# Row sums of a 16384 x 1024 array: two leads of 128 rows instead of one

## The chip, the cores and the metric

The kernel runs on one core of a Trainium2 chip. The metric is the device time of one launch in microseconds (us); where several runs are named, their median. A core has engines with instruction streams of their own: VectorE (DVE in the profile), ScalarE (ACT), GpSimd (POOL), TensorE (PE) and SyncE (SP). Data come from the chip's memory (DRAM) into the on-chip buffer, which has 128 partitions, through DMA transfers; here all of them are issued on SP, onto one queue that 16 DMA engines work through. The engines wait for each other, and for landed transfers, by semaphores.

## The reference

```python
def setup_inputs():
    batch, seq, dim = 32, 512, 1024
    return {
        "x": np.random.randn(batch, seq, dim).astype(np.float32),
        "multiplier": 0.5,
    }

def reference(x: np.ndarray, multiplier: float) -> np.ndarray:
    return (np.sum(x, axis=-1) * multiplier).astype(np.float32)
```

Each of the 16384 rows of 1024 float32 numbers is summed and multiplied by 0.5. The input has 67.11 MB, the output 65.5 KB.

## The kernel before

The rows are shared out over the 128 partitions, 128 rows to each. They are processed in blocks of B = 16 rows of a partition: 8 blocks. A full block is 64 KB in each partition, 8192 KB in all.

- Blocks 0 to 6 (loop at L114): partition p owns the 112 consecutive rows p*112 to p*112 + 111, so a block's partitions lie 448 KB apart in DRAM. Three buffers of a block each (`buf`, xb in the profile) take turns. The load of block b (`load`, L81; the issue itself is L83) waits on SP until VectorE has reduced block b - 3. VectorE sums the whole block in one instruction (`reduce_sum`, L133) into `sums` and scales the sums into `res` (L139). Of block 6 VectorE takes only the first 8 rows; ScalarE sums the other 8, one row to an instruction (`act_row`, L89, L90), with scale and sum in one.
- The lead (L113, L125 to L130): the last 128 rows of the array, one row to a partition, in one load of 512 KB that is issued ahead of all others. VectorE sums it with `dve_sum` (L98, L100), which adds one half of a row to the other and sums the result. The sums stand in a column of `lead_sq`, a tile of 128 x 32 that a memset (L111) has cleared. A transpose of 32 x 32 blocks (L128) brings them into the rows 0, 32, 64, 96 of `lead_tr`, 32 sums to a row.
- The last block has `tail` = 15 rows in a partition (partition p owns 15 consecutive rows, 60 KB apart), and comes in five loads: pieces of 9 and 4 rows (L156), a mixed one of row 13 and the first 384 columns of row 14 (`landed_mix`), and the rest of row 14 in two loads of 352 and 288 columns into the tile `end` (L169). All five wait on SP for the reduction of block 4 (L155). Rows 5 to 8 and 12 and row 13 are ScalarE's (L182, L193); the others are VectorE's, by `dve_sum`. Row 14 is summed in three parts: each partial sum is put into a column of `end` beside the next part's numbers, so the last sum, `final` (L200), contains the two before it.
- Stores: SP waits for block 6's scaled sums (L173) and stores the 112 finished sums of each partition (L174, the early store), then the lead's 128 sums as 4 rows of 32 (L178). At the end it waits for ScalarE's last row (L204) and for `final`, and stores the last block's sums (L205). L209 to L211 wait until the three stores have landed.

The function `start_loads_at_entry` puts the loads that wait for nothing (the lead and blocks 0 to 2) into the entry block on SP, ahead of the barrier at which all engines meet. So they are issued first of all; VectorE and ScalarE start after that barrier.

The order on SP is then: lead, blocks 0, 1, 2; blocks 3, 4, 5, 6, each behind its wait; the five loads of the last block; the early store; the lead's store; the last store.

Of the kernel before, what the change touches and what calls it, by code (L numbers as in the profile page):

```python
# [9 lines left out]
def kernel(  # L10
# [13 lines left out]
    nc = tc.nc  # L24
# [4 lines left out]
    P = nc.NUM_PARTITIONS  # L29
# [4 lines left out]
    N, D = x_flat.shape  # L34
    rows = N // P
    out_flat = out.rearrange("b s -> (b s)")
    mul = float(multiplier)

    B = 16
    n_blocks = rows // B  # L40
    assert N == P * rows and rows == n_blocks * B
    own = rows - B
    tail = B - 1
    lead0 = P * (own + tail)
    x_rows = x_flat[0 : P * own, :].rearrange("(p c) d -> p c d", p=P)
    x_last = x_flat[P * own : lead0, :].rearrange("(p c) d -> p c d", p=P)
    x_lead = x_flat[lead0:N, :]
    out_rows = out_flat[0 : P * own].rearrange("(p c) -> p c", p=P)
    out_last = out_flat[P * own : lead0].rearrange("(p c) -> p c", p=P)
    out_lead = out_flat[lead0:N].rearrange("(q c) -> q c", c=32)  # L50

    def sbuf(name, *shape):
        return ctx.enter_context(nc.sbuf_tensor(name, list(shape), fp32)).ap()
# [4 lines left out]
    res = sbuf("res", P, rows)  # L58
    cut = (384, 736)
    at = 352  # L60
    end = sbuf("end", P, at + 2 + D - cut[1])
    S = 32
    lead = sbuf("lead", P, D)
    lead_sq = sbuf("lead_sq", P, S)
    lead_tr = sbuf("lead_tr", P, S)

    def sem(name):
        return nc.alloc_semaphore(name=name)
# [5 lines left out]
    def marks(i, engine):  # L74

        s = dve_done if engine == "dve" else act_done
        i.then_inc(s, 1)
        counts[engine] += 1
        return counts[engine]

    def load(name, dst, src, free=None):  # L81
        landed = sem(name)
        i = nc.sync.dma_start(out=dst, in_=src)  # L83
        if free is not None:
            i.wait_op(dve_done, free, "sem-ge")
        i.then_inc(landed, 16)
        return landed

    def act_row(t, r, col):  # L89
        return nc.scalar.activation(  # L90
            out=t[:, r, :],
            in_=t[:, r, :],
            func=mybir.ActivationFunctionType.Copy,
            scale=mul,
            accum_out=res[:, col : col + 1],
        )

    def dve_sum(row, dst, scale):  # L98
        mid = row.shape[-1] // 2
        return nc.vector.tensor_tensor_reduce(  # L100
            out=row[:, 0:mid],
            in0=row[:, 0:mid],
            in1=row[:, mid:],
            scale=scale,
            scalar=0.0,
            op0=ADD,
            op1=ADD,
            accum_out=dst,
        )

    zeroed = marks(nc.vector.memset(lead_sq, 0.0), "dve")  # L111
    freed = []
    lead_landed = load("lead_landed", lead, x_lead)  # L113
    for b in range(n_blocks - 1):  # L114
        c0 = b * B
        t = buf[b % bufs]
        landed = load(
            f"landed{b}",
            t,
            x_rows[:, c0 : c0 + B, :],  # L120
            freed[b - bufs] if b >= bufs else None,
        )
        h = B if b < n_blocks - 2 else B // 2
        if b == 0:
            nc.vector.wait_ge(lead_landed, 16)  # L125
            nc.vector.wait_ge(dve_done, zeroed)
            summed = marks(dve_sum(lead, lead_sq[:, 0:1], mul), "dve")
            turned = nc.vector.transpose(out=lead_tr, in_=lead_sq)  # L128
            turned.wait_op(dve_done, summed, "sem-ge")
            marks(turned, "dve")  # L130
        nc.vector.wait_ge(landed, 16)
        done = marks(
            nc.vector.reduce_sum(  # L133
                out=sums[:, c0 : c0 + h], in_=t[:, 0:h, :], axis=mybir.AxisListType.X
            ),
            "dve",
        )
        freed.append(done)
        scaled = nc.vector.tensor_single_scalar(  # L139
            out=res[:, c0 : c0 + h],  # L140
            in_=sums[:, c0 : c0 + h],
            scalar=mul,
            op=mybir.AluOpType.mult,
        )
        scaled.wait_op(dve_done, done, "sem-ge")
        early_dve = marks(scaled, "dve")
        if h < B:
            nc.scalar.wait_ge(landed, 16)
            for r in range(h, B):
                i = act_row(t, r, c0 + r)  # L150
            early_act = marks(i, "act")
# [1 line left out]
    c0 = (n_blocks - 1) * B  # L153
    t = buf[(n_blocks - 1) % bufs]
    nc.sync.wait_ge(dve_done, freed[n_blocks - 1 - bufs])  # L155
    pieces = [(0, 9), (9, 13)]  # L156
    landed = [
        load(f"landed_p{k}", t[:, lo:hi, :], x_last[:, lo:hi, :])
        for k, (lo, hi) in enumerate(pieces)
# [15 lines left out]
    early.wait_op(act_done, early_act, "sem-ge")  # L175
    early_stored = sem("early_stored")
    early.then_inc(early_stored, 16)
    lead_store = nc.sync.dma_start(out=out_lead, in_=lead_tr[0:P:S, :])  # L178
    lead_stored = sem("lead_stored")
    lead_store.then_inc(lead_stored, 16)  # L180

    on_act = {5, 6, 7, 8, 12}  # L182
    for k, (lo, hi) in enumerate(pieces):
        on = [r for r in range(lo, hi) if r in on_act]
        nc.scalar.wait_ge(landed[k], 16)
# [11 lines left out]
    part = dve_sum(end[:, 0:at], end[:, at + 1 : at + 2], 1.0)  # L197

    part.then_inc(landed_end[1], 1)
    final = dve_sum(end[:, at:], res[:, rows - 2 : rows - 1], mul)  # L200
    final.wait_op(landed_end[1], 17, "sem-ge")
    done = marks(final, "dve")

# [3 lines left out]
    stored = sem("stored")  # L207
    store.then_inc(stored, 16)
    nc.sync.wait_ge(early_stored, 16)  # L209
    nc.sync.wait_ge(lead_stored, 16)  # L210
    nc.sync.wait_ge(stored, 16)  # L211

    def start_loads_at_entry(nc_):
# [61 lines left out]
```

## Time and profile before

| | |
|---|---|
| Time, median of 3 runs | 160.63 us (160.52 to 160.78) |
| Profiled execution, its own time | 160.85 us |
| Its span, first to last instruction | 159.5 us |
| VectorE idle before block reductions (L133), waiting for loads | 30.5 us, 7 times |
| ScalarE idle, waiting for loads | 138.8 us, 4 times |
| Read from DRAM, mean rate over the span | 67.11 MB, 421 GB/s |

The profile is of one execution. Its span is shorter than the time of the run, which also contains what lies before the first and after the last instruction. In the lines of the profile, a row of the timeline gives start, duration, engine, line, operation, output and input with their shapes, how many instructions are merged into the row, and in brackets the idle time before it and what ended it. "SPq" is the issue of a DMA on SP; its duration is that of the issue, not of the transfer. A row of the chain gives start, duration and what it was. A row of DMA issues gives how often, the size and the time from issue to landing. "CUSTOM_DVE_ANT_0" is the instruction of `dve_sum`.

### The profile page before, as it was taken

To read this page: it belongs to the slowest core of one execution; us is meant where nothing else is said; L and a number is where in the kernel's file an instruction comes from. 1 tells how busy PE (TensorE), PEld (TensorE's weight loads), DVE (VectorE), ACT (ScalarE), POOL (GpSimd) and SP (SyncE) were. 2 spreads that over 40 slices of the span, in tenths; PEclk is the share of its full clock that TensorE was granted. 3 is DMA by queue.
4 is the path that set the end of the run, shared out by engine and by line. 5 is a ranking of instruction groups with operands and counts; after the bars stand their busy time and mean duration, and the time that the engine had idled before them with its cause. 6 is when DMAs were issued, how large, how long until landed. Compare 5 with 4: busy or idle time off the path is not lost.

```text
span 159.5 us, 129 instructions
## 1 busy us (share of the span) xinstructions
DVE 120.2 (75%) x40; ACT 16.3 (10%) x29; POOL 0.2 (0%) x4
## 2 busy tenths in 40 slices
DVE  2000029999499995999869997799959999599456
ACT  2000000000000000000000000000000000099384
POOL 0000000000000000000000000000000000000000
DMA  9969979999699699699898996996996996999994
GB/s 394 526 263 526 477 312 526 394 394 526 279 509 526 263 526 493 296 526 411 378 526 362 427 526 279 509 526 263 526 526 263 526 526 263 411 444 444 407 405 141
DMA packets 2168, 67.18 MB, mean 421 GB/s; under 512 B 504, under 2 KB 760, under 8 KB 1016
## 3 DMA queue, kind: packets, MB, share of 16 engines
q1 hardware_dynamic: 2168, 67.18, 98.0%
HBM read 67.11 MB, written 0.07 MB: 421 GB/s over the span
## 4 chain that ended last, share of the span: by engine, by line
DMA 75%; DVE 24%; SPq 1%; issue 0%
DMA xb<-in_x_dram 75%; DVE sums L133 22%; DVE xb L100 1%; SPq L83 1%; DVE end L100 0%; DVE res L139 0%; DVE res L100 0%
## 5 line engine op out<-in xcount | busy, mean ns | idle before, releaser
L133 DVE TENSOR_REDUCE sums<-xb 128x16 f32<-128x16384 f32 (+1 forms) x7 | 112.0, 16001 | 30.5 <-DMA xb<-in_x_dram 30.5
L90 ACT ACTIVATE xb<-xb 128x1024 f32<-128x1024 f32 x14 | 14.6, 1045 | 138.8 <-DMA xb<-in_x_dram 138.8
L100 DVE CUSTOM_DVE_ANT_0 xb<-xb 128x512 f32<-128x512 f32 (+1 forms) x9 | 5.3, 649 | 3.8 <-DMA xb<-in_x_dram 3.8
L90 ACT ACTIVATION_READ_ACCUMULATOR xb<-xb 128x1 f32 x14 | 2.6, 187 | 0.0
L111 DVE MEMSET lead_sq<- 128x32 f32 x1 | 0.1, 85 | 2.9 <-PEq L26 2.9
L90 ACT ACT_TABLE_LOAD x1 | 1.3, 1283 | 2.9 <-PEq L26 2.9
L139 DVE TENSOR_SCALAR res<-sums 128x16 f32<-128x16 f32 (+1 forms) x7 | 1.2, 174 | 0.2
L100 DVE CUSTOM_DVE_ANT_0 lead<-lead 128x512 f32<-128x512 f32 x1 | 0.7, 692 | 0.2 <-DMA lead<-in_x_dram 0.2
L100 DVE DVE_READ_ACCUMULATOR2_ANT res<- 128x1 f32 x9 | 0.7, 81 | 0.0
L100 DVE CUSTOM_DVE_ANT_0 end<-end 128x176 f32<-128x176 f32 (+1 forms) x2 | 0.7, 328 | 0.1
L128 DVE STREAM_TRANSPOSE lead_tr<-lead_sq 128x32 f32<-128x32 f32 x1 | 0.2, 213 | 0.0
L100 DVE DVE_READ_ACCUMULATOR2_ANT end<- 128x1 f32 x2 | 0.2, 82 | 0.0
L256 POOL MEMSET const-bfloat16-1.0<- 128x1 bf16 x1 | 0.1, 101 | 0.0
L256 POOL MEMSET const-uint8-127<- 128x1 uint8 x1 | 0.1, 101 | 0.0
L256 POOL MEMSET const-float32-0.0<- 128x1 f32 x1 | 0.1, 98 | 0.2 <-issue 0.2
L256 POOL MEMSET const-float32-1.0<- 128x1 f32 x1 | 0.1, 98 | 0.0
L100 DVE DVE_READ_ACCUMULATOR2_ANT lead_sq<- 128x1 f32 x1 | 0.1, 82 | 0.0
## 6 DMA issues: line engine op xcount, KB each, us to landing
xb<-in_x_dram SPq DMA_DIRECT2D x1, 4608.0 KB, 32.4
xb<-in_x_dram SPq DMA_DIRECT2D x1, 2048.0 KB, 36.9
xb<-in_x_dram SPq DMA_DIRECT2D x1, 704.0 KB, 38.1
lead<-in_x_dram SPq DMA_DIRECT2D x1, 512.0 KB, 3.2
end<-in_x_dram SPq DMA_DIRECT2D x1, 176.0 KB, 38.1
end<-in_x_dram SPq DMA_DIRECT2D x1, 144.0 KB, 38.0
xb<-in_x_dram SPq DMA_DIRECT2D x7, 41.0
out_dram<-res SPq DMA_DIRECT2D x1, 56.0 KB, 9.6
```

The lines of the kernel that those rows point to most:

```text
L83: i = nc.sync.dma_start(out=dst, in_=src)
L90: return nc.scalar.activation(out=t[:, r, :], in_=t[:, r, :], func=mybir.ActivationFunctionType.Copy, scale=mul, accum_out=res[:, col : co ...
L100: return nc.vector.tensor_tensor_reduce(out=row[:, 0:mid], in0=row[:, 0:mid], in1=row[:, mid:], scale=scale, scalar=0.0, op0=ADD, op1=ADD, ...
L111: zeroed = marks(nc.vector.memset(lead_sq, 0.0), "dve")
L128: turned = nc.vector.transpose(out=lead_tr, in_=lead_sq)
L133: nc.vector.reduce_sum(out=sums[:, c0 : c0 + h], in_=t[:, 0:h, :], axis=mybir.AxisListType.X),
L139: scaled = nc.vector.tensor_single_scalar(out=res[:, c0 : c0 + h], in_=sums[:, c0 : c0 + h], scalar=mul, op=mybir.AluOpType.mult,)
L256: nc = _bacc.Bacc("TRN2", target_bir_lowering=False, num_devices=1)
```

## The change

The number of leads becomes L = 2. The last 256 rows of the array are the leads: two sets of 128 consecutive rows, one row to a partition, in two loads of 512 KB each, both without a wait and so both in the entry block ahead of block 0. VectorE waits for the first and sums it into column 0 of `lead_sq`, then waits for the second and sums it into column 1; one transpose serves both, which leaves the second lead's sums in rows 1, 33, 65, 97 of `lead_tr`. Each lead has a store of its own, both on one semaphore.

The last block has 14 rows in a partition, 56 KB apart. Its first piece has 8 rows instead of 9; the second still has 4, and the mixed one and the two ends keep their sizes, all one row earlier. ScalarE's rows move with them (4 to 7 and 11, then 12), so VectorE sums 4 rows of the first piece instead of 5, and ScalarE 4 as before. The last store has 14 sums of each partition instead of 15.

In the order of instructions, SP has one load more after the first, and one lead store more after the lead's store; VectorE has one `dve_sum` more ahead of the transpose and one fewer in the first piece; ScalarE's are the same. Lines behind the change move down by up to six.

```diff
-    tail = B - 1
+    L = 2
+    tail = B - L
...
-    out_lead = out_flat[lead0:N].rearrange("(q c) -> q c", c=32)
+    out_lead = out_flat[lead0:N].rearrange("(l q c) -> l q c", l=L, c=32)
...
-    lead = sbuf("lead", P, D)
+    lead = sbuf("lead", P, L, D)
...
-    lead_landed = load("lead_landed", lead, x_lead)
+    lead_landed = [
+        load(f"lead_landed{l}", lead[:, l, :], x_lead[l * P : (l + 1) * P, :])
+        for l in range(L)
+    ]
...
         if b == 0:
-            nc.vector.wait_ge(lead_landed, 16)
             nc.vector.wait_ge(dve_done, zeroed)
-            summed = marks(dve_sum(lead, lead_sq[:, 0:1], mul), "dve")
+            for l in range(L):
+                nc.vector.wait_ge(lead_landed[l], 16)
+                summed = marks(dve_sum(lead[:, l, :], lead_sq[:, l : l + 1], mul), "dve")
...
-    pieces = [(0, 9), (9, 13)]
+    pieces = [(0, 8), (8, 12)]
...
-    lead_store = nc.sync.dma_start(out=out_lead, in_=lead_tr[0:P:S, :])
     lead_stored = sem("lead_stored")
-    lead_store.then_inc(lead_stored, 16)
-
-    on_act = {5, 6, 7, 8, 12}
+    for l in range(L):
+        lead_store = nc.sync.dma_start(out=out_lead[l], in_=lead_tr[l:P:S, :])
+        lead_store.then_inc(lead_stored, 16)
+
+    on_act = {4, 5, 6, 7, 11}
...
-    final = dve_sum(end[:, at:], res[:, rows - 2 : rows - 1], mul)
+    final = dve_sum(end[:, at:], res[:, own + tail - 1 : own + tail], mul)
...
-    nc.sync.wait_ge(lead_stored, 16)
+    nc.sync.wait_ge(lead_stored, 16 * L)
```

## The prediction

> **What bounds the kernel now.** I read the page first (busy times, DMA share, chain of waits), then the chain in order of time, then the timeline at both ends of the span, and last the DMA share in short windows at the start. The page:
>
> ```profile
> DVE 120.2 (75%) x40; ACT 16.3 (10%) x29; POOL 0.2 (0%) x4
> ...
> q1 hardware_dynamic: 2168, 67.18, 98.0%
> ...
> DMA 75%; DVE 24%; SPq 1%; issue 0%
> ```
>
> The one DMA queue keeps its 16 engines occupied for 98.0% of the span; no compute engine passes 75%. The chain gives DMA 75%, and its 24% of DVE are reductions that free a buffer for a load already far ahead, so they too stand beside a running transfer stream. The end of the chain:
>
> ```profile
> 118.17 36.88 DMA xb<-in_x_dram
> ...
> 155.08 0.69 DVE xb L100
> ...
> 157.27 0.40 DVE end L100 x3
> ...
> 157.70 0.31 DVE end L100
> ```
>
> From 155.08, where the second piece of the last block has landed, VectorE runs almost without a break to 158.01; the last 288 columns land at about 157.6 (issued near 119.6, 38.0 to landing), so stream and VectorE reach the last sum together. Both hang on the stream's position, since 155.08 is itself a landing. The starts of work are the landings that the rest of the working uses; first the opening, then the later landings:
>
> ```profile
> 0.00 0.39 SPq L83 DMA_DIRECT2D lead<-in_x_dram  x1
> ...
> 0.44 1.37 SPq L83 DMA_DIRECT2D xb<-in_x_dram  x3
> ...
> 3.20 0.69 DVE L100 CUSTOM_DVE_ANT_0 lead<-lead 128x512 f32<-128x512 f32 x1 [0.16 <-DMA lead<-in_x_dram]
> ...
> 22.89 17.22 DVE L133 TENSOR_REDUCE sums<-xb 128x16 f32<-128x16384 f32 x1 [18.75 <-DMA xb<-in_x_dram]
> ```
>
> ```profile
> 42.34 17.22 DVE L133 TENSOR_REDUCE sums<-xb 128x16 f32<-128x16384 f32 x1 [2.02 <-DMA xb<-in_x_dram]
> ...
> 139.26 8.69 DVE L133 TENSOR_REDUCE sums<-xb 128x8 f32<-128x8192 f32 x1 [1.92 <-DMA xb<-in_x_dram]
> ...
> 148.63 0.63 SPq L178 DMA_DIRECT2D out_dram<-lead_tr  x1
> 150.18 1.06 ACT L90 ACTIVATE xb<-xb 128x1024 f32<-128x1024 f32 x1 [2.50 <-DMA xb<-in_x_dram]
> ...
> 155.08 0.69 DVE L100 CUSTOM_DVE_ANT_0 xb<-xb 128x512 f32<-128x512 f32 x1 [1.74 <-DMA xb<-in_x_dram]
> ...
> 156.82 1.06 ACT L90 ACTIVATE xb<-xb 128x1024 f32<-128x1024 f32 x1 [0.59 <-DMA xb<-in_x_dram]
> ...
> 158.04 0.34 SPq L205 DMA_DIRECT2D out_dram<-res  x1
> ```
>
> Every one of these VectorE and ScalarE starts was released by a DMA, after idle time: 18.75 us before the first block, about 2 before the others, 1.74 before the second piece. Work waits for bytes all the way.
>
> **The rate, from the landings.** Blocks 1 to 6 land between 42.34 and 139.26: five intervals in 96.92 us, 19.38 us for a block of 8192 KB. The first piece (4608 KB) takes 150.18 - 139.26 = 10.92, the second (2048 KB) 155.08 - 150.18 = 4.90, the mixed one (704 KB) 156.82 - 155.07 = 1.75. Block against second piece: 6144 KB more in 14.48 us more is 424.3 KB/us, which leaves 4.90 - 2048/424.3 = 0.07 us for a transfer as such. The first piece bears it out: 4608/424.3 + 0.07 = 10.93, seen 10.92. The mixed piece, with the shorter run of 5.5 KB in each partition, leaves 1.75 - 704/424.3 = 0.09. The two end pieces together take at most 157.67 - 156.82 = 0.85 for 320 KB (0.75 by the rate), so at most 0.05 each.
>
> **The change, part by part.**
>
> *Bytes.* One row of each partition, 512 KB, 1.21 us by the rate, leaves the first piece of the last block and becomes the second lead. The total is the same, so on a stream that never stops this is 0. All landings between move later by that 1.21 us and by what the extra transfer costs: the first block from 22.89 to about 24.2, block 6 from 139.26 to 140.56, and the first piece, 512 KB smaller, is back at about 150.27.
>
> *One more load (L83, on SP).* The second lead has 4 KB in each partition; no row shows that in the middle of the stream. Nearest is the mixed piece: +0.09. Lower bound 0: there is one transfer more and no byte less, and no row has a piece quicker than its bytes. Upper bound 0.31: the first block's work starts 22.89 - 3.20 = 19.69 after the lead's, 0.31 more than a block's interval of 19.38, were all of that due to a short transfer in front. I take 0.09, since 5.5 KB is nearest to 4 KB and the other rows (0.05, 0.07) stand round it.
>
> The first lead's start to landing is 3.2 us, of which 1.21 are bytes, so about 2.0 us are set-up and receipt that a lone transfer pays; behind another one it shows as the 0.05 to 0.09 above. The Trainium skill, "DMA: Bandwidth & Descriptors", section "Anatomy of one DMA — SWDGE (gpsimd) path", speaks against this change: it fits each transfer, on GpSimd's path, as about 2.0 us fixed plus bytes at 436 GB/s, which is an estimate of 3.2 us for a lead, and the trace's single lead agrees with 3.2. Its "Rules for kernel authors" say that the fixed part overlaps when a transfer is issued early. Paid in line, the sum would be 2.0 us up instead of 0.09; the landings of the pieces speak for the second reading.
>
> *SP at the start.* The second lead's issue takes the slot from 0.44 to about 0.88, and the three block issues move back by 0.44. The engines' first packets are the test of the cover:
>
> ```profile
> 0.80:1.20 0.40, 0.00 (x0) 0.00 (x0) 0.00 (x0) 1.00 0.39 102
> 1.20:1.60 0.40, 0.00 (x0) 0.00 (x0) 0.00 (x0) 1.00 0.96 328
> ```
>
> The last two columns are DMA share and GB/s: 0.39 of the first window is used, so packets begin near 1.05, 0.66 after the first issue ends at 0.39. The second lead's would be ready near 0.88 + 0.66 = 1.54, the first lead's bytes last to 1.05 + 1.21 = 2.26: 0.7 us of cover. The first block's packets, ready near 2.0, have until 3.5. Cost 0; without the cover, 0.44. The entry loads also end 0.44 later on SP, and VectorE's first instruction (memset, at 2.95 after the entry's barrier) may move from 2.95 to 3.4. It has until 24.2.
>
> *VectorE.* One more row sum (0.69, and 0.08 to read the accumulator) after the second lead lands at about 4.5, and the transpose behind it, done by 5.5: inside the 18.75 us of idle. One row fewer in the first piece, four instead of five at 0.615 apart (150.18, 150.80, 151.41...): the piece's sums end near 152.7 instead of 153.3, and then wait for the second piece at 155.17. Gain 0, as it only lengthens the 1.74 us of idle. Block 6's half reduction (8.69) and its scaling (0.17) end near 149.45 instead of 148.15, before the first piece at 150.27. 0.8 us of idle are left of 2.03, and ScalarE keeps 1.3 of its 2.50. The rows after the second piece are the same in number and kind.
>
> *Buffers.* Block 3's load waits for the first reduction, which ends near 41.4 instead of 40.1, while blocks 1 and 2 are queued until 43.6 and 63; the same lead of one block and more holds for each later load, the last block's included. Cost 0; it would take a delay of some 20 us to empty the queue.
>
> *Stores.* The early store waits on SP (L173) for block 6's scaling, and goes near 149.5 instead of 148.24. Behind it on SP stand now two lead stores of 0.63 each, to about 151.1; the next thing there waits until 158. The page on these transfers:
>
> ```profile
> lead<-in_x_dram SPq DMA_DIRECT2D x1, 512.0 KB, 3.2
> ...
> out_dram<-res SPq DMA_DIRECT2D x1, 56.0 KB, 9.6
> ...
> out_dram<-res SPq DMA_DIRECT2D x1, 7.5 KB, 1.4
> ```
>
> The early store lands at 148.24 + 9.6 = 157.84, just after the last load, since it is queued behind the loads. The lead stores come after it, and the added one moves 0.5 KB, 4 rows of 128 bytes; the last store is issued at 158.04 + 0.09 in any case. Cost 0, upper bound 1.4, if the last store had to sit out one more store's landing. The last store's rows are 56 bytes instead of 60: 0.
>
> *Sum.* 0 + 0.09 = +0.09 us. The profiled execution took 160.85 us, 159.5 of span and 1.35 around it, so 160.94 for the like of it. It stands 0.22 above the median of the runs, 160.63; for the median, 160.72, told as 160.7.
>
> **The rivals.**
>
> *An opening gap (slower).* If the engines run dry between the leads, the added issue of 0.44 us is paid in full: 160.63 + 0.09 + 0.44 = 161.2. It decides when the first lead's packets end before the second's are ready, which by the windows is 0.7 us off; for it speaks the 0.31 us that the first block is late already. 0.12.
>
> *The tail's first piece runs slower.* Its rows are now 32 KB in a partition, 56 KB apart, instead of 36 KB, 60 KB apart. At the mixed piece's rate (704/1.75 = 402 KB/us) its 4096 KB take 10.19 instead of 9.72: +0.47, so 161.2. Against it: 36 KB and 16 KB runs, and blocks whose partitions lie 448 KB apart, all fit one rate. 0.05.
>
> *The second lead store delays the last one:* +1.4, 162.1. Against it: some 0.5 us pass between the early store's landing and the last issue's end. 0.05.
>
> *The queue takes transfers one after another:* +2.0, 162.7. The pieces' 0.07 say no. 0.03.
>
> *The removed row counts (faster).* If VectorE's work behind the first piece set the end, one row less is 0.61 off: 160.0. For it speaks that VectorE runs without a break after 155.08; against it the 1.74 us of idle just before. 0.11.
>
> **How the numbers follow.** What this kernel's measurement can tell from no change is about 0.2%, 0.32 us. The forecast (0 to 0.31 up) has 0.64, the four slower cases 0.25, the faster one 0.11. The range takes in the forecast with the runs' own spread (160.52 to 160.78) and the two cases at 161.2, and leaves out 160.0, 162.1 and 162.7, together 0.19: 160.3 to 161.2.
>
> **What would show it right or wrong.** Right: the first block's reduction starts near 24.2, block 6's near 140.6, the first piece's rows near 150.3, the second's near 155.2, the last sum near 157.8; VectorE idles about 2.4 before the second piece and 0.8 before the first. The opening gap would show as a first block later than 24.5 and windows with a DMA share well under 0.9 between 2.0 and 3.0; a slow tail as more than 9.9 us between block 6 and the first piece; the stores as a last landing more than 1.6 after its issue. A first piece that lands as forecast with a last sum before 157.3 would make the faster rival true and my reading of the end wrong.

## The result, and the profile after

The changed kernel takes 161.95 us in the median of 17 runs (160.67 to 162.19), the kernel before 160.58 in 17 runs (160.52 to 160.9): a ratio of 1.0064, 95% interval 1.0048 to 1.0079. It is slower, and above the forecast's range, which ended at 161.2. The runs are not spread evenly: five of the 17 lie at 160.67 to 161.0, the others at 161.42 to 162.19, and the profiled execution, at 162.01 (span 160.7), is one of the latter.

The page of the changed kernel, in the lines that were shown of before (busy time of the engines, the DMA queue, the chain by engine):

```profile
DVE 120.3 (75%) x40; ACT 16.3 (10%) x29; POOL 0.2 (0%) x4
...
q1 hardware_dynamic: 2320, 67.18, 97.5%
...
DMA 75%; DVE 22%; SPq 1%; ACT 1%; issue 0%
```

These totals hide the loss. The queue has the same 67.18 MB, the compute engines the same work, and the DMA share falls by half a per cent. The loss shows in the timeline (start, duration, engine, line, operation; in brackets the idle time before):

```profile
0.00 0.87 SPq L84 DMA_DIRECT2D lead<-in_x_dram  x2
...
0.91 1.42 SPq L84 DMA_DIRECT2D xb<-in_x_dram  x3
...
3.47 0.09 DVE L112 MEMSET lead_sq<- 128x32 f32 x1 [3.47 <-PEq L26]
...
4.56 0.69 DVE L101 CUSTOM_DVE_ANT_0 lead<-lead 128x512 f32<-128x512 f32 x1 [0.27 <-DMA lead<-in_x_dram]
...
25.23 17.22 DVE L138 TENSOR_REDUCE sums<-xb 128x16 f32<-128x16384 f32 x1 [19.72 <-DMA xb<-in_x_dram]
```

```profile
141.49 8.69 DVE L138 TENSOR_REDUCE sums<-xb 128x8 f32<-128x8192 f32 x1 [1.93 <-DMA xb<-in_x_dram]
...
151.21 0.69 DVE L101 CUSTOM_DVE_ANT_0 xb<-xb 128x512 f32<-128x512 f32 x1 [0.82 <-DMA xb<-in_x_dram]
...
156.11 0.69 DVE L101 CUSTOM_DVE_ANT_0 xb<-xb 128x512 f32<-128x512 f32 x1 [2.36 <-DMA xb<-in_x_dram]
...
158.73 0.31 DVE L101 CUSTOM_DVE_ANT_0 end<-end 128x145 f32<-128x145 f32 x1
159.13 0.34 SPq L211 DMA_DIRECT2D out_dram<-res  x1
```

The second lead's sum starts at 4.56, as forecast (4.5). The first block starts at 25.23, 1.0 us behind the forecast 24.2. From there on every distance is as it was: six block intervals in 141.49 - 25.23 = 116.26 us, 19.38 each; the first piece 9.72 behind block 6 (forecast 9.71), the second piece 4.90 behind the first. So, but for 0.1 us at the last store, all that is lost is lost between the second lead and the end of the first block, and it is never made up.

The end itself, in the chain of waits (start, duration, what) and in the DMA issues (size, time from issue to landing):

```profile
120.86 37.02 DMA xb<-in_x_dram
...
157.91 1.15 ACT xb L91 x2
```

```profile
out_dram<-res SPq DMA_DIRECT2D x1, 56.0 KB, 8.4
...
out_dram<-res SPq DMA_DIRECT2D x1, 7.0 KB, 1.5
```

The chain now leaves the stream at the mixed piece (157.91) and goes through ScalarE's last row, to 159.06; VectorE's last sum, from 158.73 to 159.04 and its read of the accumulator, ends with it. It is the same close finish as before, one microsecond later.

Where in the first block, the DMA share in short windows shows (the last two columns are DMA share and GB/s). A packet is booked whole into the window in which it starts, which is why shares pass 1. A packet of a block has 64 KB, so 164 GB/s in a window of 0.4 us is one packet. First the end of the first block in the changed kernel:

```profile
23.40:23.80 0.40, 0.00 (x0) 0.00 (x0) 0.00 (x0) 1.00 3.81 1638
23.80:24.20 0.40, 0.00 (x0) 0.00 (x0) 0.00 (x0) 1.00 1.15 492
24.20:24.60 0.40, 0.00 (x0) 0.00 (x0) 0.00 (x0) 1.00 0.00 0
24.60:25.00 0.40, 0.00 (x0) 0.00 (x0) 0.00 (x0) 1.00 1.14 492
```

10 and 3 packets start between 23.4 and 24.2, the next ones of 13 engines; then nothing; then 3 packets between 24.6 and 25.0. Three of the 16 engines are 1 us behind. In the kernel before the same place has all 16 within 0.8 us:

```profile
21.80:22.20 0.40, 0.00 (x0) 0.00 (x0) 0.00 (x0) 1.00 3.05 1311
22.20:22.60 0.40, 0.00 (x0) 0.00 (x0) 0.00 (x0) 1.00 3.04 1311
```

The delay has its origin at the first block's first packets. The view of the DMA queue counts packets by size for a stretch of time. The packets under 8 KB, the leads' 4 KB and some of a few bytes, are called short below; all packets counted less the short ones are the block's. For the changed kernel, first the stretch from 1 to 5 us, then from 1 to 5.6:

```profile
DMA packets 302, 1.97 MB, mean 492 GB/s; under 512 B 32, under 2 KB 32, under 8 KB 288
```

```profile
DMA packets 304, 2.10 MB, mean 456 GB/s; under 512 B 32, under 2 KB 32, under 8 KB 288
```

By 5 us, 302 - 288 = 14 engines have begun the first block; the last two begin only between 5.4 and 5.6, though the second lead's sums were already possible at 4.56. The third late engine has begun by 5 and loses its time inside its first packet: 13 second packets start between 6.4 and 7.2, then none, then 3 between 7.6 and 8.0. In the kernel before all 16 engines have begun the block by 3.0 (160 - 144). An engine carries its own part of every load, and a load has landed when all 16 parts have. With every engine occupied from then on, an engine that starts 1 us late ends 1 us late, and each landing waits for it.

### The profile page after: what moved, and what is told of

It reads as the page before. It is cut to its first block, busy times and chain, and to the rows that moved or that the text cites. A ratio compares the mean times of both kernels' runs of the same rounds, so it can differ in the third digit from the quotient of the medians.

```text
span 160.7 us, 131 instructions
## 1 busy us (share of the span) xinstructions
DVE 120.3 (75%) x40; ACT 16.3 (10%) x29; POOL 0.2 (0%) x4
## 2 busy tenths in 40 slices
DMA packets 2320, 67.18 MB, mean 418 GB/s; under 512 B 528, under 2 KB 784, under 8 KB 1168
## 3 DMA queue, kind: packets, MB, share of 16 engines
q1 hardware_dynamic: 2320, 67.18, 97.5%
## 4 chain that ended last, share of the span: by engine, by line
DMA 75%; DVE 22%; SPq 1%; ACT 1%; issue 0%
DMA xb<-in_x_dram 75%; DVE sums L138 21%; SPq L84 1%; ACT xb L91 1%; DVE res L144 0%
## 5 line engine op out<-in xcount | busy, mean ns | idle before, releaser
L101 DVE CUSTOM_DVE_ANT_0 xb<-xb 128x512 f32<-128x512 f32 (+1 forms) x8 | 4.7, 646 | 3.2 <-DMA xb<-in_x_dram 3.2
L101 DVE CUSTOM_DVE_ANT_0 lead<-lead 128x512 f32<-128x512 f32 x2 | 1.4, 692 | 0.3 <-DMA lead<-in_x_dram 0.3
```

The costliest lines, as they stand in the source:

```text
L101: return nc.vector.tensor_tensor_reduce(out=row[:, 0:mid], in0=row[:, 0:mid], in1=row[:, mid:], scale=scale, scalar=0.0, op0=ADD, op1=ADD, ...
```

## The experiments

A load's place in the order of SP is what the edits change. Each was run beside the kernel before on the same chip, whose median in the four groups of runs was 160.56 to 160.59. The first four ask what part of the change costs the time.

**E1, the changed kernel again.** No edit.

> The changed kernel again, unedited, for a second trace. In the first one the first block lands 1.04 us later than forecast (25.23, not 24.19) and everything behind it keeps its forecast distances; 3 of the 16 engines are about 1 us behind the others at the end of the first block. All theories: a median near 162.0, and where a trace shows a span near 160.7 the first block starts near 25.2, where it shows one near 159.5 the first block starts near 24.2.

Measured: 161.96 (160.63 to 162.28), ratio 1.0070 (1.0046 to 1.0094). The second trace, of a run at 162.2, has the first block at 25.47. By 4.4 us 12 engines have begun it, the last of them between 5.0 and 5.4. The number of late engines is not fixed.

**E2, both leads in one load.** The same 256 packets of 4 KB, one load fewer:

```diff
-    lead_landed = [
-        load(f"lead_landed{l}", lead[:, l, :], x_lead[l * P : (l + 1) * P, :])
-        for l in range(L)
-    ]
+    both = load("lead_landed", lead, x_lead.rearrange("(l p) d -> p l d", l=L))
+    lead_landed = [both] * L
```

> Both leads in one load of 1024 KB, the same 4 KB packets, one load fewer in the queue. Theory COUNT (the added load in the opening costs the stall, by its issue or by its own end on every engine): median 160.6 to 160.9, first block near 24.2. Theory BYTES or TIMING (the short packets reach beyond 4 us, and meet there what goes on at the start): still near 162.0, first block near 25.2.

Measured: 160.82 (160.71 to 161.29), ratio 1.0013 (1.0004 to 1.0021). The wait is gone, with the tail of 14 rows, the two lead stores and all bytes in place. The time is COUNT's, and the tail is cleared. The first block:

```profile
24.33 17.22 DVE L136 TENSOR_REDUCE sums<-xb 128x16 f32<-128x16384 f32 x1 [17.67 <-DMA xb<-in_x_dram]
```

24.33 is 0.14 from the 24.19 that the forecast's working gives for the change. The windows of this kernel have the 16 first packets together (2724 GB/s are 16 packets and the last of the lead's):

```profile
4.20:4.60 0.40, 0.00 (x0) 0.26 (x1) 0.00 (x0) 1.00 6.36 2724
```

**E3, the kernel before with its lead in two loads.** Nothing else of the change:

```diff
-    lead_landed = load("lead_landed", lead, x_lead)
+    lead_landed = [
+        load(f"lead_landed{l}", lead[:, lo : lo + D // 2], x_lead[:, lo : lo + D // 2])
+        for l, lo in enumerate((0, D // 2))
+    ]
```

> The kernel before, its one lead in two loads of 512 columns, 256 KB each: one load more in the opening, no byte more, the tail as it was. Theory COUNT: near 161.7, the first block near 24.0 instead of 22.89. Theory BYTES or TIMING: 160.6 to 160.8, the first block near 22.9 to 23.0.

Measured: 163.05 (161.58 to 163.29), ratio 1.0138 (1.0110 to 1.0166). One load more with no byte more costs 2.5 us, more than the change itself. The direction is COUNT's, its size (near 161.7) is not. That the price grows where the short packets end sooner (by 3.5 here, by 4.3 in the change) is a guess that E5 does not bear out. The trace is of the run at 161.58 and so does not show what the median pays.

**E4, the second lead behind the first block.** In the loop, `load_lead(1)` follows the load of block 0; its sum comes before block 1's:

```diff
+    lead_landed = [load_lead(0)]
...
         if b == 0:
+            lead_landed.append(load_lead(1))
             nc.vector.wait_ge(dve_done, zeroed)
...
+        if b < L:
+            nc.vector.wait_ge(lead_landed[b], 16)
+            summed = marks(dve_sum(lead[:, b, :], lead_sq[:, b : b + 1], mul), "dve")
```

> The changed kernel with the second lead loaded behind the first block, not ahead of it; five loads ahead of the barrier and the tail of 14 rows as in the change. Theory that the five loads or the tail cost the time: near 162.0. Theory that the second lead between the first and the first block costs it: 160.6 to 160.9, with the first block near 22.9 and the second near 43.6.

Measured: 160.95 (160.82 to 161.35), ratio 1.0023 (1.0013 to 1.0033), just past the expected band. Five loads ahead of the barrier are not the reason; the second lead's place ahead of the first block is. The first two blocks:

```profile
22.82 17.22 DVE L141 TENSOR_REDUCE sums<-xb 128x16 f32<-128x16384 f32 x1 [18.49 <-DMA xb<-in_x_dram]
...
43.45 17.22 DVE L141 TENSOR_REDUCE sums<-xb 128x16 f32<-128x16384 f32 x1 [2.36 <-DMA xb<-in_x_dram]
```

Their distance is 20.63, 1.25 more than an interval of 19.38, for 1.21 us of bytes: in mid-stream the added load costs 0.04 us beyond its bytes.

The next four ask whether the wait grows with the number of loads (SUPPLY) or ends at a certain time (HELD).

**E5, the kernel before with its lead in four loads** of 256 columns each (as E3, with a step of `D // 4`).

> The kernel before, its one lead in four loads of 256 columns, 128 KB each, so the first block is the fifth load. Theory SUPPLY (in the opening each load's packets become ready on the last engines only 1.3 to 2 us behind those of the load before, and the engines wait for them): the two halves of the run before cost 2.5, four quarters cost 4 to 6.5, 164.6 to 167, with the first block's work starting near 27 to 29. Theory HELD (some engines are held until about 5.45 us after the start, whatever is queued): no worse than the halves, at most 163.3, first block at most near 25.5.

Measured: 163.22 (162.69 to 163.47), ratio 1.0160 (1.0144 to 1.0175), the first block at 25.81. Four loads cost no more than two: SUPPLY, with a price for each load, falls. HELD fits the time, if not quite the first block (25.5 at most). The short packets end by 4.1, much as in the change, and yet the price is nearly twice as high. Nor is any engine late to begin: by 4.6 all 16 have begun the first block (592 packets less 576 short ones). But 14 second packets start between 6.6 and 7.8, and the last two only between 8.2 and 8.6. In this trace two engines lose the time inside their first packet, not ahead of it.

**E6, three leads, one and then two rows to a partition** (L = 3, pieces of 7 and 4 rows, ScalarE's rows moved to match):

```diff
+    lead_landed = [load("lead_landed0", lead[:, 0, :], x_lead[0:P, :])]
+    rows2 = x_lead[P : L * P, :].rearrange("(l p) d -> p l d", l=2)
+    lead_landed += [load("lead_landed1", lead[:, 1:L, :], rows2)] * 2
```

> Three leads in two loads, one row and then two rows to a partition, with a tail of 13 rows: the same number of loads ahead of the first block as in the change, but short packets until about 4.9 us instead of 3.8 to 4.2. Were the added load alone the price, near 162.0. Both SUPPLY with a price for each load and HELD have about 0.5 us left of the wait: 161.1 to 161.5. SUPPLY with a price for each packet: 162.5 or more.

Measured: 160.82 (160.63 to 161.05), ratio 1.0015 (1.0006 to 1.0024): better than any theory said. As many loads stand ahead of the first block as in the change, but the short packets last longer; the first block's packets start between 5.0 and 5.8 with nothing to wait for:

```profile
4.60:5.00 0.40, 0.00 (x0) 0.12 (x1) 0.00 (x0) 1.00 0.97 389
5.00:5.40 0.40, 0.00 (x0) 0.00 (x0) 0.00 (x0) 1.00 3.90 1649
5.40:5.80 0.40, 0.00 (x0) 0.00 (x0) 0.00 (x0) 1.00 3.11 1342
```

So the count of loads by itself is not the price: E6, with two loads, takes no longer than E2 with one. A second load seems to cost when the engines run out of short packets too early; E9, E14 and E15 below do not all fit that.

**E7, both leads behind the first block, and E8, the kernel before with its lead behind the first block.** The lead loads move below the load of block 0, their sums ahead of block 1's.

> The changed kernel with both leads behind the first block. No engine comes to a load's end before 20 us, so by SUPPLY and HELD no wait is left: 160.5 to 160.9, the first block near 21.6. If two short loads in a row cost the time wherever they stand, near 162.

> The kernel before with its one lead behind the first block. The first packets of the first block take up to 0.3 us more than later ones in the kernel before; if that is the same wait in small, 160.2 to 160.5, and if it belongs to any first long packet, 160.5 to 160.7.

Measured: E7 161.12 (160.88 to 161.26), ratio 1.0032 (1.0020 to 1.0045); E8 160.81 (160.72 to 161.01), ratio 1.0015 (1.0006 to 1.0023). Neither has the wait of the change. Both are 0.1 to 0.2 above what was expected, and neither beats the kernel before. E7's first block is at 21.91 (expected near 21.6); E8's:

```profile
21.88 17.22 DVE L134 TENSOR_REDUCE sums<-xb 128x16 f32<-128x16384 f32 x1 [18.71 <-DMA xb<-in_x_dram]
```

Without the lead's 1.21 us ahead of it, 21.68 was to be had (22.89 - 1.21); a block in front begins 0.2 us worse than a lead in front.

Four more runs test reasons for the late packets.

**E9, one load for both leads, then a load of 64 bytes to a partition.** E2 with

```diff
+    small = sbuf("small", P, 16)
+    small_landed = load("small_landed", small, x_lead[0:P, 0:16])
```

> Both leads in one load as in e2, and behind it a load of 64 bytes to a partition (8 KB in all, its data unused), so that the first block is third in order again while the short packets end as in e2, near 4.5 us. Theory THIRD (the third load's packets reach some engines only near 5.45 us): 161.2 to 161.9, first block near 25.0 to 25.3. Theory HELD (what is queued, and its order, is no matter): as e2, 160.7 to 160.95, first block near 24.4.

Measured: 161.10 (160.90 to 161.19), ratio 1.0032 (1.0020 to 1.0044), between the two bands. The trace decides against THIRD: the first block is third in order, and by 5 us all 16 engines have begun it (432 packets less 416 short ones), with its work at 24.55, 0.2 behind E2's. HELD falls with it, as 16 engines are not held until 5.45 here, nor in E2, where all have begun by 4.6.

**E10, the change without ScalarE's rows.** `act_row` is not called, `res` is cleared by a memset, and SP does not wait for ScalarE; 14 rows of each partition are not summed.

> The changed kernel without ScalarE's work: its 14 rows of a partition are left out (their sums stay at a memset's zeros), and with them the table that ScalarE loads at 3.39 to 4.67 us. Were that table's load what holds the engines: 160.5 to 160.9, first block near 24.2. THIRD: no different from the change, a median near 161.9, first block near 25.2.

Measured: 161.58 (160.69 to 161.90), ratio 1.0049 (1.0032 to 1.0066). In the trace, of a run at 161.9, no table is loaded, the first block is at 25.53, and one engine begins it behind 5.0. The table is not what holds the engines.

**E11, the change with blocks 1 and 2 issued behind the barrier:**

```diff
-            freed[b - bufs] if b >= bufs else None,
+            freed[b - bufs] if b >= bufs else zeroed if b else None,
```

> The changed kernel with the loads of blocks 1 and 2 issued behind the barrier, after VectorE's memset, so that only the two leads and the first block are queued at the start. If the issue of the later blocks holds up the first block's packets: 160.6 to 160.9, first block near 24.2. If the first block's own place in the order is the reason: near 162.0 and 25.2.

Measured: 162.04 (161.74 to 162.31), ratio 1.0087 (1.0074 to 1.0100), the first block at 25.38. The later blocks' issues have no part in it.

**E12, the kernel before with E9's small load between the lead and the first block.**

> The kernel before with a load of 64 bytes to a partition (8 KB, its data unused) between the lead and the first block. THIRD: the short packets end near 2.6, the first block's reach some engines near 5.45: 162.5 to 163.3, first block near 25.5. If the bytes of two short loads are needed for the loss: 160.6 to 160.8, first block near 23.0.

Measured: 163.20 (162.91 to 163.25), ratio 1.0161 (1.0147 to 1.0174), the first block at 25.37 instead of 22.89. 8 KB cost 2.6 us. No theory of bytes is left. The view of the queue from 1 to 5.26 us:

```profile
DMA packets 303, 1.52 MB, mean 356 GB/s; under 512 B 160, under 2 KB 160, under 8 KB 288
```

303 - 288 = 15: a single engine begins the first block behind 5.26 (by 5.27 it is counted), while the lead's sum was possible at 3.66 at the latest. At the end of the first block it is still alone:

```profile
22.20:22.60 0.40, 0.00 (x0) 0.00 (x0) 0.00 (x0) 1.00 4.19 1802
22.60:23.00 0.40, 0.00 (x0) 0.00 (x0) 0.00 (x0) 1.00 1.52 655
```

11 and 4 packets start there, the next ones of 15 engines, and then none until 24.6. One engine late is enough for the whole price.

The last three were to narrow down the cause.

**E13, the small load of one single partition** in the place of E12's.

> The kernel before with a load of 64 bytes of one single partition (data unused) between the lead and the first block: the first block is issued as late as in e12, but only one of the 16 engines has a part in the load between. If being issued near 1 us instead of 0.44 is what makes its packets late: near 163.2 as e12, first block near 25.4. If the engines' own third load is what counts: 160.6 to 160.9, first block near 22.9 to 23.2, or one engine late at most.

Measured: 162.95 (162.52 to 163.22), ratio 1.0142 (1.0126 to 1.0158), the first block at 25.34. In the trace, again one engine is late; from 1 to 4.5 us:

```profile
DMA packets 161, 1.51 MB, mean 431 GB/s; under 512 B 18, under 2 KB 18, under 8 KB 146
```

161 - 146 = 15 engines have begun, though the block was issued as late for all of them as for the sixteenth. 64 bytes of one partition are enough. But the run does not decide between the two theories: the time is the first one's, and one late engine is the most that the second allowed. Against the second speaks E12, where the small load has 128 packets, one for every partition, and one engine alone is late all the same. Against the first speaks the trace of E15 below, where the block is issued as late (0.91) and no engine is late. The trace does not name engines, so that the late one is the one with the small load is not shown.

**E14, E9 with packets of 8 KB** (two consecutive rows to a partition: `x_lead.rearrange("(p l) d -> p l d", l=L)`).

> As e9, but the leads' one load brings 2 consecutive rows to a partition, 128 packets of 8 KB where e9 has 256 of 4 KB; the lead sums come out in another order. The short packets end near 3.7 us. If the 256 packets of e9's load were its protection: a wait until 5.3 to 5.6, 162.2 to 162.7, first block near 26. If not: 160.8 to 161.2, first block near 24.2 to 24.6.

Measured: 161.56 (161.04 to 162.10), ratio 1.0055 (1.0038 to 1.0072), the first block at 24.98. It falls between the bands. All engines have begun by 5 us, so in this trace it is not the change's wait of single engines. The trace is of the slowest of the six runs (162.10); against E9's it has the first block 0.43 later, and the last store lands 2.0 us after its issue instead of 1.5, so half of what it has more than E9 lies at the end. It leaves E9's protection unexplained.

**E15, the small load ahead of the lead.**

> The kernel before with e12's load of 64 bytes to a partition ahead of the lead, not behind it. If any two short loads ahead of the first block make its packets late: 162.9 to 163.3, first block near 25.4. If the load between a short one and a long one has to be the small one: 160.6 to 161.0, first block near 23.2.

Measured: 161.49 (161.25 to 161.96), ratio 1.0058 (1.0043 to 1.0074). The trace, of a run at 161.31, has the first block at 23.38, 0.49 late, and no late engine by 5 us. Of that, 0.44 is the lead's issue, now second (0.44 instead of 0.00): the stream itself starts later. So the two short loads of E12 in the other order do not make its wait in this trace; what the slower runs of E15 (up to 161.96) pay for, it does not show.

## Why the prediction was wrong, by its own steps

*The bound, the bytes and the rate: right.* DMA sets the end before and after; the intervals of 19.38 and the pieces at 9.72 and 4.90 are the forecast's. With that the rival of a slower tail falls (it needed more than 9.9), and so does that of a queue that takes one transfer after another.

*One more load, 0.09: right in size.* E4 has 0.04 for it in mid-stream, within the bounds of 0 and 0.31. E2, which has the whole change but for the count of loads, is 0.23 above before (160.82 to 160.59), so on the forecast's side of the 0.32 that was called measurable.

*SP at the start, "0.7 us of cover. Cost 0": this step failed.* It took the first load's 0.66 us from issue to packets and gave the same to the loads behind it. The window behind the 0.66 was misread, as its 102 GB/s are ten packets counted whole and not a part of the window in use; that the first packet does start between 1.00 and 1.05, by a narrower window, makes the value right by luck. It held for the second lead: the windows from 1.8 to 3.4 have no gap (shares of 0.97 to 1.10). It did not hold for the first block, which was issued by 1.34, was to be ready near 2.0, and was not there on two engines until after 5.4, 4.1 us behind its issue. The cover was larger than the forecast's 1.5 us (from 2.0 to 3.5), since the leads' packets last longer: by 3.5 the queue's view has 230 short ones, by 4.3 all 288. Even these 2.2 us or so were not enough; the late engines would have needed 3.4. The rows of before had shown readiness for one load alone, with nothing under way; no row showed it for a later one, and there the step should have had two bounds.

*The opening gap as a rival* named the place (a first block behind 24.5) and had 0.12. Its price of 0.44, one issue, and its point, a gap between the leads, were wrong: the gap lies behind the second lead, on some engines alone, and costs 1.0. The range, up to 161.2, ends 0.75 below the median.

*VectorE, buffers, barrier: right.* The memset is at 3.47 (forecast 3.4), the idle times before the pieces are 0.82 and 2.36 (0.8 and 2.4), and the removed row bought nothing, as the chain's end said.

*Stores: nearly.* The two lead stores took 1.19 us of SP, unnoticed. The last store landed 1.5 us after its issue, not 1.4. With the first block's 1.04 over the forecast, 0.09 for the load and these 0.1, the span's 1.2 us (160.7 to 159.5) are accounted for.

The sum, then: a term of +0.09 that holds, and a term of 0 that was +1.0 in the profiled execution. Between the medians the change costs 1.37 (161.95 to 160.58), and E2, with both leads in one load, 0.23. The five of its 17 runs at 160.67 to 161.0 lie where E2 lies, so the loss seems to be absent in some runs; none of these five has a trace.

What stays open is why the first block's packets come late, and to which engines. Shown is: 1.4 to 2.6 us were lost in the kernels with two or more short loads ahead of the first block whose packets end by about 4.3 (the change, E3, E5, E12, E13), and not in E6 and E9, where they last beyond 5 and to about 4.8. The second may be 64 bytes of one partition (E13). The bytes, the later blocks' issues and ScalarE's table are not the reason (E12, E11, E10), and the loss is absent when the same packets come in one load (E2), or with a long load in between (E4). The end of the short packets is not the whole condition: E15's end by 3.5, and it costs 0.9 and not 2.6; E14's end near 4.8 as E9's do, and it costs 1.0 where E9 costs 0.5. Nor is a late start the only form: in E5's trace the time goes inside the first packet. That every third load is late until about 5.3 is refuted by E9, and what protects E9 is not known: E14, which was to tell, fell between. The Trainium skill, "DMA: Bandwidth & Descriptors", section "Latency and other measured facts", gives about 0.6 us to the first byte for transfers issued on SP; the first lead's 0.61 to 0.66 agrees, the first block's 4.1 on the late engines does not, and here the measurement decides.

No version that was run beats the kernel before. If two leads are wanted, one load for both (E2) costs 0.13% where the change costs 0.64%.

## What to carry to other kernels

In the opening of a stream like this one, be wary of one short load behind another ahead of the first long one: 8 KB there cost 2.6 us, while two leads joined into one load, or with a long load between or ahead of them, cost 0.2 to 0.5. It is not a rule without exception (E6 cost 0.2), so the order of the first loads is to be tried. Where all DMA engines are occupied to the end, a delay of a single engine at the start is paid in full, and the page's shares do not show it; count the packets that have begun in short windows. And where readiness of a load is taken from one row, ask whether that row had the same loads ahead of it.

## What was not expected of the hardware

One engine of 16 that begins its first long packet late (E12: 15 have begun by 4.5, the last behind 5.26) costs the whole program 2.6 us. The time from the last store's issue to its landing is not constant: 1.4 us in before, E2 and E8, 1.7 in E7, and 2.0 in E14 and in E4, whose last sum starts at 157.42, 0.28 earlier than in before, and whose profiled execution is yet 0.31 longer (161.16 to 160.85). What sets it was not tried.
